# Sums of weight quarters: by VectorE subtractions before, by accumulating transfers from GpSimd after

## The chip, the cores and the metric

The kernel runs on one core of one Trainium2 chip. The metric is the device time of one execution, in microseconds (us). Before the change it is 1552.88 us, the median of 3 runs (1552.12 to 1553.69). The engines are TensorE (PE: matrix products; PEld is its weight load), VectorE (DVE), ScalarE (ACT), GpSimd (POOL) and SyncE (SP). Products are summed in PSUM; operands stand in SBUF. Transfers are carried out by 16 DMA engines and issued from the queue of an engine, in this kernel from SP and ACT.

## The reference

One layer of a decoder: a norm, two parallel token mixers fed by one input projection, an output projection, then a norm, a gated MLP with a causal convolution, and a last norm. There are 256 positions, D_MODEL is 2048 and D_FF is 5632, all in float32. The change lies in the last product, by w_down:

```python
h = rmsnorm(x, norm_ffn_w[l])
gate, up = jnp.split(jnp.einsum('bsd,df->bsf', h, w_up[l]), 2, axis=-1)
gate = causal_dwconv(gate, conv_ffn_w[l]) + conv_ffn_b[l]
x = x + jnp.einsum('bsf,fd->bsd', jax.nn.gelu(gate, approximate=False) * up, w_down[l])
return rmsnorm(x, norm_final_w)
```

## The kernel before

Float32 products are made of three products of parts: each operand is split into a high part (rounded to the type that TensorE takes) and a low part (what is left), and high times high, low times high and high times low are summed. A weight tile is [128, 2, 512], 256 rows of the weight by 512 columns, 512 KB. `srcs` is the list of all weight tiles in the order of their use. `load` issues the transfer of a tile on SP (line 157, four buffers `raw`). `begin` splits it: ScalarE casts it to the high part `whi` (line 209), then VectorE subtracts that from the tile, which gives `wlo` (line 217). `whi` and `wlo` have three buffers each, so a tile is split when TensorE has finished with the tile three places before. `weights` hands out the next tile and keeps two more split ahead (`AHEAD`).

The down projection is the last stage, from about 1311 us of the span. The activations are [256 positions, 5632], kept as 11 chunks of 512 features. It runs in two halves of 1024 output columns (`hf`), each with eight direct chunks and three chunks in `SEVEN`. A direct tile ("plain") is used for both position blocks: 12 matmuls. A chunk in `SEVEN` is a 2 by 2 by 2 block product made with seven products instead of eight: the weight block [512, 1024] of the chunk is loaded as two `quad` tiles of 1 MB (rows 0 to 255 and 256 to 511, line 167, buffers `x1` and `x2`), whose column halves are the quarters b11, b12, b21 and b22. The activations likewise have four blocks a11 to a22, and `half_sums` makes four sums of these, S1 to S4, and splits them.

The seven products come in the order of `PRODUCTS`: 11, 21, 22, T1, T3, T2, T4. The first three take a quarter as it is. For the others VectorE first replaces a quarter by a difference (line 204), in place: T1 in b11, T3 in b12, T2 in b22 and T4 in b21. The result is then split like any other tile. Each of the seven is used in 6 matmuls, and `stream` puts one plain tile behind each but the first. So a group is 11, 21, plain, 22, plain, T1, plain, T3, plain, T2, plain, T4, plain; there are three groups per half, six in all, with 4, 2 and 2 plain tiles ahead of the groups in the first half and 3, 1 and 1 in the second. Products 21, 22 and T4 are summed straight into the output's banks; 11, T1, T2 and T3 have banks of their own, which are combined once per half, after the last group (`u2`, `u3`, lines 1296 to 1304). A new group's quads are loaded when the buffers are free: the first when T1 and T3 of the group before are split, the second when T2 and T4 are.

The order of the instructions on each engine is set when the kernel is built, by a scheduler; each engine runs its list in order and waits on semaphores.

Of the kernel before, what the change touches and what calls it, by code (L numbers as in the profile page):

```python
# [12 lines left out]
ALU = mybir.AluOpType  # L13
# [22 lines left out]
def kernel(  # L36
# [20 lines left out]
    nc = tc.nc  # L57
# [11 lines left out]
    def nm(s):  # L69
        cnt[0] += 1  # L70
        return f"{s}_{cnt[0]}"

    def pg(shape=(P, 512)):
        return psg.tile(list(shape), F32, tag="g", name=nm("psg"))
# [70 lines left out]
    def weights(ahead=AHEAD):  # L145

        begin(taken[0] + ahead + 1)
        taken[0] += 1
        return made[taken[0] - 1]
# [11 lines left out]
    def quarter(half, chunk, what):  # L161

        if what == "11":
            for j in range(2):
                r = big.tile([P, 2, 1024], F32, tag=f"x{1 + j}", name=nm("quad"))
                rows = slice((2 * chunk + j) * 256, (2 * chunk + j + 1) * 256)
                last_load[0] = nc.sync.dma_start(r, w_down[0, rows, half * 1024 : (half + 1) * 1024]
                                                 .rearrange("(k p) f -> p k f", p=P)).ins
                for i in range(2):
                    quarters[j, i] = r[:, :, 512 * i : 512 * (i + 1)]  # L170
        b11, b12, b21, b22 = (quarters[j, i] for j in range(2) for i in range(2))
        sums = {"T1": (b11, b12, b11), "T3": (b12, b22, b12), "T2": (b22, b22, b11), "T4": (b21, b21, b22)}
        return sums[what] if what in sums else quarters[int(what[0]) - 1, int(what[1]) - 1]

    def load(n):
        while len(loads) < min(len(srcs), n):
            m = len(loads)
            for k in range(2) if m < HALVES else (slice(None),):
                load_part(m, k)
# [18 lines left out]
    def begin(n):  # L198
        while len(made) < min(len(srcs), n):
            load(len(made) + 1)  # L200
            raw = loads[len(made)]
            if isinstance(raw, tuple):
                raw, plus, minus = raw
                nc.vector.tensor_tensor(raw, plus, minus, op=ALU.subtract)
            shape = list(raw.shape)
            keep = kept.get(len(made))
            hi = wpool.tile(shape, F32R, tag="whi", name=nm("whi")) if keep is None else \
                mtile(keep, shape, F32R, nm("khi"))
            nc.scalar.copy(hi, raw)  # L209
            if shape[1] == 8:  # L210
                lo = None
                nc.vector.tensor_tensor(hi[:, :, 32:64], raw[:, :, 0:32], hi[:, :, 0:32].bitcast(F32),
                                        op=ALU.subtract)
            else:
                lo = wpool.tile(shape, F32R, tag="wlo", name=nm("wlo")) if keep is None else \
                    mtile(4 + keep, shape, F32R, nm("klo"))
                last_split[0] = nc.vector.tensor_tensor(lo, raw, hi.bitcast(F32), op=ALU.subtract).ins  # L217
                splits.append(last_split[0])
            made.append((hi, lo))
# [11 lines left out]
    def pm():  # L231
        return psm.tile([P, 2, 512], F32, tag="m", name=nm("psm"))
# [81 lines left out]
    def mtile(i, shape, dt, name):  # L314
        return big.tile(shape, dt, tag=f"m{i}", name=name)
# [207 lines left out]
    for g, w in enumerate(WINDOWS):  # L523
# [12 lines left out]
                            op=ALU.add)  # L536
# [29 lines left out]
    s1 = mp.tile([P, 2, NH], F32, name="s1")  # L566
# [3 lines left out]
    s2 = mp.tile([P, 2, NH], F32, name="s2")  # L570
# [602 lines left out]
    def half_sums(c):  # L1173

        h = whole[c]
        a11, a12, a21, a22 = (h[:, 2 * j : 2 * j + 2, t * P : (t + 1) * P] for t in range(2) for j in range(2))
        s = fp.tile([P, 4, S], F32, tag="y", name=nm("sums"))
        s1, s2, s3, s4 = (s[:, n].rearrange("p (k s) -> p k s", k=2) for n in range(4))
        nc.vector.tensor_tensor(s1, a21, a22, op=ALU.add)
        nc.vector.tensor_tensor(s2, s1, a11, op=ALU.subtract)  # L1180
        nc.vector.tensor_tensor(s3, a11, a21, op=ALU.subtract)
        nc.vector.tensor_tensor(s4, a12, s2, op=ALU.subtract)
        if c == SEVEN[1]:
            hi, lo = (lambda b: (b[:, 0], b[:, 1]))(big.tile([P, 2, 4, S], F32R, tag="x3", name="sx"))
        else:
            more = dict(tag="gs", bufs=2) if c == SEVEN[2] else {}
            hi, lo = (fp.tile([P, 4, S], F32R, name=f"s{n}{c}", **more) for n in ("hi", "lo"))
        nc.scalar.copy(hi, s)
        nc.vector.tensor_tensor(lo, s, hi.bitcast(F32), op=ALU.subtract)
        sums_of[c] = (hi, lo)  # L1190
# [53 lines left out]
    def products(ps, high, low, w, first, last, cs=slice(0, 512), shared=False):  # L1244
        for kk in range(2):
            for n, (part_, lhs) in enumerate(((w[0], high), (w[0], low), (w[1], high))):
                mm(ps[:, cs], lhs(kk), part_[:, kk, cs], start=(first and kk == 0 and n == 0),  # L1247
                   stop=(last and kk == 1 and n == 2), skip_group_check=shared)

    def direct(ps, kp, t, w, first, last, **more):  # L1250
        products(ps, lambda kk: lh(2 * kp + kk, t), lambda kk: ll(2 * kp + kk, t), w, first, last, **more)
# [4 lines left out]
    for hf in range(2):  # L1256
        if hf == 0:
            own = [pm() for c in range(2)]
            own = {(c, t): own[c][:, t] for c in range(2) for t in range(2)}
            other = [pg() for n in range(4)]  # L1260
        else:
            own = {(c, t): pg() for c in range(2) for t in range(2)}
            other = [p[:, t] for p in (pm(), pm()) for t in range(2)]
        bank_of = dict(zip(("11", "T1", "T2", "T3"), other))
        bank_of |= {"21": own[0, 0], "22": own[1, 0], "T4": own[0, 1]}
        began = set()
        for n, step in enumerate(steps[hf]):
            w = weights()
            if step[0] == "keep":
                wk.append(w)  # L1270
                continue
            if step[0] == "plain":
                kp, c = step[1], step[2] % 2
                more = any(x[0] == "plain" and x[2] % 2 == c for x in steps[hf][n + 1 :]) or hf == 1
                for t in range(2):
                    direct(own[c, t], kp, t, w, (c, t) not in began, not more, shared=hf == c == t == 1)
                    began.add((c, t))
                continue
            chunk, what = step[1:]
            if hf == 0 and what == "11" and chunk != SEVEN[-1]:  # L1280
                half_sums(SEVEN[SEVEN.index(chunk) + 1])
            which = OPERAND[what]
            if isinstance(which, tuple):
                high, low = (lambda kk, f=f, j=which[0], t=which[1], chunk=chunk: f(4 * chunk + 2 * j + kk, t)
                             for f in (lh, ll))
            else:
                high, low = (lambda kk, s=s, which=which: s[:, which, kk * P : (kk + 1) * P] for s in sums_of[chunk])
            ps = bank_of[what]
            alone = what in ("11", "T1", "T2", "T3")
            products(ps, high, low, w, alone and what not in began, alone and chunk == SEVEN[-1])  # L1290
            began.add(what)
            if chunk == SEVEN[-1] and what == PRODUCTS[-1]:
                c0, c1 = 2 * hf, 2 * hf + 1
                u = fp.tile([P, 2, 512], F32, tag="y", name=nm("u"))
                u2, u3 = u[:, 0], u[:, 1]
                nc.scalar.copy(u2, bank_of["11"])
                plus(0, c0, bank_of["11"])
                nc.vector.tensor_tensor(u2, u2, bank_of["T2"], op=ALU.add)
                nc.vector.tensor_tensor(u3, u2, bank_of["T3"], op=ALU.add)
                plus(1, c0, u3)  # L1300
                nc.vector.tensor_tensor(u2, u2, bank_of["T1"], op=ALU.add)
                plus(0, c1, u2)
                nc.vector.tensor_tensor(u3, u3, bank_of["T1"], op=ALU.add)
                plus(1, c1, u3)
        if hf == 0:
            for c in range(2):
                for t in range(2):
                    plus(t, c, own[c, t])
                    squared(t, c, c)
                    weighted(t, c)  # L1310
# [90 lines left out]
```

## Time and profile before

| What | Value |
|---|---|
| Median of 3 runs | 1552.88 us (1552.12 to 1553.69) |
| The profiled execution | 1552.15 us |
| Its span in the profile | 1550.4 us |
| Down projection's first matmul | at 1311.3 us of the span |
| VectorE's operations on line 204 | 24, each 1.22 us |
| Loads of quads | 12, 1 MB each |
| Issues from GpSimd's queue | none |

The profile is one execution. Its page has the busy time of each engine (a matmul counts from its start to a modelled end, so neighbours overlap), the span in 40 slices, the chain of work that ended last, the costliest groups of instructions and the transfers. Other views of the same trace are used too: the timeline (start and duration in us, engine, line, operation, output and inputs, and in brackets the idle time before it and what ended it), busy times in stretches of the span, a line's instructions with what its engine waited for (in total us, times), and the transfers by line with their size and the median time from issue to landing.

### The profile page before, as it was taken

The page shows a single profiled execution, that of the slowest core. Times are in us where ns is not written, and L with a number is a line of the kernel's source. Part 1 is how long each engine was busy: PE and PEld are TensorE (multiplying, and loading weights), DVE is VectorE, ACT ScalarE, POOL GpSimd, SP SyncE. Part 2 cuts the span into 40 slices and gives each one's busy share as a digit, 9 for nine tenths or more (in the row PEclk, how much of TensorE's full clock was granted, in tenths as well). Part 3 has the DMA queues.
Part 4 walks back from the last instruction along what each step waited for, and adds up shares of the span by engine and source line. Part 5 has one row for each costly group of instructions (what it writes and reads, how often), then busy time and mean ns, then how long its engine had stood idle before and what let it go on. Part 6 is the DMA issues. An engine that isn't in the chain of part 4 may idle for free.

```text
span 1550.4 us, 21200 instructions
## 1 busy us (share of the span) xinstructions
PE 1541.6 (99%) x7942; PEld 1294.1 (83%) x7942; DVE 1151.4 (74%) x1749; ACT 770.3 (50%) x987; POOL 39.3 (3%) x54
## 2 busy tenths in 40 slices
PE   9999999999999999999999999999999999999998
PEld 8888888788888888888888888888888888888886
DVE  6788858996689858886656667767666677877885
ACT  6445446454545446454554544444444444555552
POOL 1010001000100000000000000000000000000000
PEclk9999999999999999999999999999999999999999
DMA  8776757776576756675656666666666668557662
GB/s 274 214 219 206 204 152 223 215 209 183 170 237 202 208 164 202 217 206 175 215 181 185 187 186 188 189 190 189 184 195 186 187 189 271 176 190 231 201 209 93
DMA packets 165846, 306.34 MB, mean 198 GB/s; under 512 B 19138, under 2 KB 23010, under 8 KB 165614
## 3 DMA queue, kind: packets, MB, share of 16 engines
q1 hardware_dynamic: 162720, 299.95, 64.2%
q10 hardware_dynamic: 3022, 5.03, 1.0%
q8 instruction: 62, 1.02, 0.3%
q14 instruction: 42, 0.34, 0.1%
HBM read 299.66 MB, written 5.28 MB: 197 GB/s over the span
## 4 chain that ended last, share of the span: by engine, by line
PE 98%; issue 1%; DMA 1%; DVE 0%; ACT 0%; POOL 0%; POOLq 0%; ACTq 0%
PE psm L250 15%; PE psm L248 15%; PE psm L249 15%; PE psm L272 11%; PE psg L272 11%; PE psm L1247 7%; PE psg L1247 7%; PE psg L273 5%; PE psm L273 5%; PE psm L391 1%; PE psg L293 1%; PE psg L781 1%; PE psg L783 0%; DMA vrow<-ev 0%; PE psm L309 0%
## 5 line engine op out<-in xcount | busy, mean ns | idle before, releaser
L209 ACT CAST whi<-raw 128x1024 fp32r<-128x1024 f32 x500 | 526.0, 1052 | 612.9 <-PE psm L249 281.8
L217 DVE TENSOR_TENSOR wlo<-raw,whi 128x1024 fp32r<-128x1024 f32 x498 | 607.3, 1222 | 287.6 <-ACT whi L209 284.5
L250 PE MATMUL psm<-wlo,xhl 128*128 128x512 f32 x864 | 339.7, 393 | 0.6 <-DVE wlo L217 0.6
L248 PE MATMUL psm<-whi,xhl 128*128 128x512 f32 x864 | 338.6, 392 | 0.0
L249 PE MATMUL psm<-whi,xhl 128*128 128x512 f32 x864 | 337.9, 391 | 0.0
L272 PE MATMUL psm<-fhl,whi 128*128 128x512 f32 x704 | 246.1, 396 | 0.0
L272 PE MATMUL psg<-fhl,whi 128*128 128x512 f32 x704 | 238.2, 395 | 0.0
L273 PE MATMUL psm<-fhl,wlo 128*128 128x256 f32 x704 | 194.3, 279 | 0.0
L250 PEld LDWEIGHTS psm<-wlo,xhl 128*128 128x128 f32 x864 | 162.2, 188 | 35.1 <-DVE wlo L217 1.9
L249 PEld LDWEIGHTS psm<-whi,xhl 128*128 128x128 f32 x864 | 162.3, 188 | 33.4
L248 PEld LDWEIGHTS psm<-whi,xhl 128*128 128x128 f32 x864 | 162.3, 188 | 33.3 <-issue 0.2
L273 PE MATMUL psg<-fhl,wlo 128*128 128x256 f32 x704 | 178.9, 280 | 0.0
L272 PEld LDWEIGHTS psm<-fhl,whi 128*128 128x128 f32 x704 | 131.3, 188 | 30.4
L272 PEld LDWEIGHTS psg<-fhl,whi 128*128 128x128 f32 x704 | 129.2, 188 | 24.3
L273 PEld LDWEIGHTS psg<-fhl,wlo 128*128 128x128 f32 x704 | 132.5, 188 | 6.9
L273 PEld LDWEIGHTS psm<-fhl,wlo 128*128 128x128 f32 x704 | 132.6, 188 | 1.2
L209 ACT CAST whi<-quad 128x1024 fp32r<-128x1024 f32 x42 | 44.3, 1054 | 47.5 <-PE psm L1247 27.6
L217 DVE TENSOR_TENSOR wlo<-quad,whi 128x1024 fp32r<-128x1024 f32 x42 | 51.3, 1222 | 18.0 <-ACT whi L209 17.3
L1247 PE MATMUL psm<-whi,hhi 128*128 128x512 f32 (+1 forms) x150 | 58.0, 387 | 0.0
L1247 PE MATMUL psm<-whi,hlo 128*128 128x512 f32 (+1 forms) x150 | 58.0, 386 | 0.0
L1247 PE MATMUL psm<-wlo,hhi 128*128 128x512 f32 (+1 forms) x150 | 57.8, 386 | 0.0
L248 PE MATMUL psm<-whi,mhi 128*128 128x512 f32 x128 | 50.9, 397 | 0.0
(323 smaller groups left out, 1699.4 us busy)
## 6 DMA issues: line engine op xcount, KB each, us to landing
raw<-in_w_in_dram SPq DMA_DIRECT2D x224, 512.0 KB, 4.2
raw<-in_w_up_dram SPq DMA_DIRECT2D x176, 512.0 KB, 4.5
raw<-in_w_down_dram SPq DMA_DIRECT2D x64, 512.0 KB, 4.6
raw<-in_w_out_dram SPq DMA_DIRECT2D x32, 512.0 KB, 3.8
quad<-in_w_down_dram SPq DMA_DIRECT2D x12, 1024.0 KB, 6.2
mv<-vrow SPq DMA_DIRECT2D x12, 512.0 KB, 4.4
taps<-in_conv_qkv_w_dram SPq DMA_DIRECT2D x16, 256.0 KB, 6.5
raw<-in_pool_w_dram SPq DMA_DIRECT2D x8, 512.0 KB, 3.9
```

Source lines behind the costliest of these rows:

```text
L209: nc.scalar.copy(hi, raw)
L217: last_split[0] = nc.vector.tensor_tensor(lo, raw, hi.bitcast(F32), op=ALU.subtract).ins
L248: mm(ps[:, t, :], lh(k, t), hi[:, kk, :], start=(k == 0), stop=False)
L249: mm(ps[:, t, :], ll(k, t), hi[:, kk, :], start=False, stop=False)
L250: mm(ps[:, t, :], lh(k, t), lo[:, kk, :], start=False, stop=(k == nk - 1))
L272: mm(ps[f], hi[:, kk, fs], rhl(k), start=(k == 0), stop=False, skip_group_check=True)
L273: mm(ps[f][:, 1, :], lo[:, kk, fs], rhl(k)[:, 0, :], start=False, stop=(k == nk - 1), skip_group_check=True)
L293: nc.tensor.transpose(pt[:, ff, t * P : (t + 1) * P], src[:, t, f * P : (f + 1) * P], ident)
L391: mm(ps_k0[:, t, :], part(k, t), w[:, kk, :], start=(k == 0 and w is hi and part is xh), stop=(k == KD - 1 and w is lo))
L781: mm(pg0, kq[:, h, 0, 0:P], kq[:, h, :, :], start=True, stop=True)
L1247: mm(ps[:, cs], lhs(kk), part_[:, kk, cs], start=(first and kk == 0 and n == 0), stop=(last and kk == 1 and n == 2), skip_group_check=shared)
```

## The change

The four differences become sums, each added in place by a transfer from GpSimd's queue that accumulates onto its destination. The signs are moved to the sums of the activations (S1 and S4) and to the combination at the end of each half. The seven products, their order in `PRODUCTS`, the loads, the splits and the matmuls are as before. The third element of the tuples in `quarter` goes away, since the first quarter is now both operand and destination: T1 = b11 + b12 in b11, T3 = b12 + b22 in b12, T2 = b22 + T1 in b22, T4 = b21 + T2 in b21.

```diff
@@ in quarter
-        sums = {"T1": (b11, b12, b11), "T3": (b12, b22, b12), "T2": (b22, b22, b11), "T4": (b21, b21, b22)}
+        sums = {"T1": (b11, b12), "T3": (b12, b22), "T2": (b22, b11), "T4": (b21, b22)}
@@ in begin
             if isinstance(raw, tuple):
-                raw, plus, minus = raw
-                nc.vector.tensor_tensor(raw, plus, minus, op=ALU.subtract)
+                raw, other = raw
+                nc.gpsimd.dma_start(raw, other, accum_op=ALU.add)
@@ in half_sums
-        nc.vector.tensor_tensor(s1, a21, a22, op=ALU.add)
+        nc.vector.tensor_tensor(s1, a21, a22, op=ALU.subtract)
         nc.vector.tensor_tensor(s2, s1, a11, op=ALU.subtract)
         nc.vector.tensor_tensor(s3, a11, a21, op=ALU.subtract)
-        nc.vector.tensor_tensor(s4, a12, s2, op=ALU.subtract)
+        nc.vector.tensor_tensor(s4, a12, s2, op=ALU.add)
@@ at the end of each half
-                nc.vector.tensor_tensor(u2, u2, bank_of["T1"], op=ALU.add)
+                nc.vector.tensor_tensor(u2, bank_of["T1"], u2, op=ALU.subtract)
                 plus(0, c1, u2)
-                nc.vector.tensor_tensor(u3, u3, bank_of["T1"], op=ALU.add)
+                nc.vector.tensor_tensor(u3, bank_of["T1"], u3, op=ALU.subtract)
                 plus(1, c1, u3)
```

## The prediction

> **What bounds the kernel now.** I read the page first, for the engine that has no idle time.
>
> ```profile
> span 1550.4 us, 21200 instructions
> PE 1541.6 (99%) x7942; PEld 1294.1 (83%) x7942; DVE 1151.4 (74%) x1749; ACT 770.3 (50%) x987; POOL 39.3 (3%) x54
> PEclk9999999999999999999999999999999999999999
> PE 98%; issue 1%; DMA 1%; DVE 0%; ACT 0%; POOL 0%; POOLq 0%; ACTq 0%
> ```
>
> TensorE is busy 99% of the span at full granted clock and is 98% of the chain of waits. The change touches only the down projection, from about 1311 us on, so I asked for the busy times of that stage in stretches of 30 us, for the twelve plus twelve vector operations that the change takes away, and for what TensorE waits for on its line there.
>
> ```profile
> 1310.00:1340.00 30.00, 30.00 (x136) 24.76 (x135) 29.10 (x34) 17.86 (x20) 0.00 (x0) 1.00 0.52 175
> 1340.00:1370.00 30.00, 30.00 (x134) 24.86 (x133) 22.14 (x19) 15.84 (x15) 0.00 (x0) 1.00 0.64 214
> ...
> 1490.00:1520.00 30.00, 30.00 (x134) 24.86 (x133) 26.25 (x27) 16.64 (x17) 0.00 (x0) 1.00 0.52 172
> ```
>
> ```profile
> L204 DVE TENSOR_TENSOR quad<-quad x12: 1216/1224/1228, 1319.9 to 1498.6; 128x1024 f32<-128x1024 f32 x12
> L204 DVE TENSOR_TENSOR quad<-quad,quad x12: 1215/1218/1226, 1323.3 to 1497.3; 128x1024 f32<-128x1024 f32 x12
> ```
>
> ```profile
>   ACT whi L209: 0.4, 2
>   DVE wlo L217: 0.4, 2
> ```
>
> In the stretches the columns are TensorE, its weight loads, VectorE, ScalarE and GpSimd busy, then the clock, the DMA share and GB/s. TensorE is busy for all of each stretch, and in the whole stage it waits 0.8 us for split weights. So nothing that VectorE sheds is worth time here, and the stage has no reserve either: a microsecond that TensorE once waits is not won back, because it has no idle time to win it from.
>
> **What is removed.** 24 subtractions of 1.22 us are 29.3 us of VectorE. They lie beside TensorE work (the stretches above), so I count them at 0. Removing them could return at most the 0.8 us of waits.
>
> **What is added.** 24 transfers, four per group, issued by GpSimd, each adding one 512 KB quarter onto another. GpSimd's queue has nothing else in this stage (0.00 in the stretches), so nothing is held up behind them but the two tiny operations at the end. But the four form a chain: T1 adds b12 to b11, T3 then overwrites b12, T2 reads the new b11 and overwrites the b22 that T3 read, T4 reads the new b22. In the built kernel's instruction order every second, third and fourth transfer of a group waits for the one before to land, and the first for the VectorE half of quarter 11's split, since it overwrites that quarter. The question is how long one link L, from issue to the issue of the next, may be. The timeline of the second group gives it: VectorE's split of 11 and of 22, ScalarE's casts of T1, T3, T2 and T4, VectorE's split of T4, and TensorE's first matmuls on T4.
>
> ```profile
> 1349.15 1.23 DVE L217 TENSOR_TENSOR wlo<-quad,whi 128x1024 fp32r<-128x1024 f32 x1 [1.27 <-ACT whi L209]
> ...
> 1355.95 1.23 DVE L217 TENSOR_TENSOR wlo<-quad,whi 128x1024 fp32r<-128x1024 f32 x1
> ...
> 1372.27 1.22 DVE L217 TENSOR_TENSOR wlo<-quad,whi 128x1024 fp32r<-128x1024 f32 x1 [1.49 <-ACT whi L209]
> ```
>
> ```profile
> 1359.17 1.06 ACT L209 CAST whi<-quad 128x1024 fp32r<-128x1024 f32 x1 [1.89 <-PE psm L1247]
> ...
> 1363.02 1.05 ACT L209 CAST whi<-quad 128x1024 fp32r<-128x1024 f32 x1 [1.66 <-PE psm L1247]
> ...
> 1367.10 1.05 ACT L209 CAST whi<-quad 128x1024 fp32r<-128x1024 f32 x1 [1.21 <-PE psm L1247]
> ...
> 1371.18 1.05 ACT L209 CAST whi<-quad 128x1024 fp32r<-128x1024 f32 x1 [1.66 <-PE psm L1247]
> ```
>
> ```profile
> 1375.29 0.39 PE L1247 MATMUL psm<-whi,hhi 128*128 128x512 f32 x1
> 1375.52 0.39 PE L1247 MATMUL psm<-whi,hlo 128*128 128x512 f32 x1
> 1375.74 0.39 PE L1247 MATMUL psm<-wlo,hhi 128*128 128x512 f32 x1
> ```
>
> The split of 11 ends at 1349.15 + 1.23 = 1350.38. The casts of T1, T3, T2 and T4 start 8.8, 12.6, 16.7 and 20.8 us later, released by TensorE giving a buffer back. Each has a cushion before TensorE suffers: T4's low half must be done when its first low matmul starts at 1375.74, and it ends at 1372.27 + 1.22 = 1373.49, so the cast may come 2.25 us later. The chain is therefore free as long as L is at most 11.0 us for T1, 2L at most 14.9 for T3, 3L at most 19.0 for T2 and 4L at most 23.05 for T4. (The split of 22, done at 1357.18, is over before 2L for any L above 3.4 us.) T4 decides: the limit is L = 5.76 us, and beyond it TensorE stalls 4L − 23.05 per group, whether the wait shows at T2 or at T4. What is late next in a stall, on ScalarE behind the waiting cast, is the next plain tile, which TensorE needs only after the late one. The last group has the same measure, 1510.06 − 1489.26 = 20.8 us:
>
> ```profile
> 1488.03 1.23 DVE L217 TENSOR_TENSOR wlo<-quad,whi 128x1024 fp32r<-128x1024 f32 x1
> ```
>
> ```profile
> 1510.06 1.05 ACT L209 CAST whi<-quad 128x1024 fp32r<-128x1024 f32 x1 [1.62 <-PE psg L1247]
> ```
>
> So I take all six groups alike: the change costs 24L − 138 us for L above 5.76, and nothing below. SyncE's queue also hangs on the chain: the reload of the second pair of quarters waits for T4's split, and plain loads queue behind it. When T4 is late, TensorE is late too, so in the first three groups this is free; in the last three, with one plain tile between groups, it may add some tenths, which I leave out.
>
> **What is L?** No accumulating transfer and none issued by GpSimd stands in the trace, so I bound it by the nearest rows, transfers by size with their median time from issue to landing, and GpSimd's smallest operation in this stage.
>
> ```profile
> raw<-in_w_down_dram SPq DMA_DIRECT2D x64, 512.0 KB, 4.6
> raw<-in_w_out_dram SPq DMA_DIRECT2D x32, 512.0 KB, 3.8
> quad<-in_w_down_dram SPq DMA_DIRECT2D x12, 1024.0 KB, 6.2
> vrow<-ev SPq DMA_DIRECT2D x4, 512.0 KB, 4.4
> ```
>
> ```profile
> L1365 POOL TENSOR_TENSOR rsf<-rsf,epsx 128x1 f32<-128x1 f32 x2 | 1.1, 550 | 722.0 <-DVE rsf L1363 722.0
> ```
>
> Lower end: the addition comes free within a plain 512 KB copy, 3.8 us. Upper end: the destination is fetched, and only then written, in two passes of 4.4 us, 8.8 us, and more if it also shares the engines. Between them: an addition must fetch two operands of 512 KB, so it is nearest to the 1024 KB load of the same stage, 6.2 us. GpSimd makes its descriptors in software; I add 0.5 us for that, from its 0.55 us operation. I take L = 6.7 us, nearer to the 1024 KB row than to either end, because two operands must pass in any case while the wait between the passes is a guess.
>
> The sum: 24 × 6.7 − 138 = 22.8 us on the profiled execution's 1552.15 us (span 1550.4), 1575 us; the median of the runs, 1552.88, is 0.7 above that execution, which changes nothing at this size. The other edits are free: the signs in the four sums of activations and the operand order in the combination leave the same number of instructions of the same size.
>
> The Trainium skill has one more doubt about the length of a link: "SBUF — State Buffer", section "Who interferes with whom", says that GpSimd can be shut out of making descriptors while VectorE runs in a mode that takes both ports, and that an operation with two tensor inputs has no such mode. The VectorE rows of this stage are of that kind, so by this rule nothing is added; without the exemption a transfer could wait out one operation of 1.22 us, and the sum would be 24 × 7.9 − 138 = 52 us instead of 23.
>
> **Rivals.** First, *the transfers are hidden*: L stays under 5.76 us. For it: the shortest 512 KB landing is 3.8 us and a second 512 KB costs 6.2 − 4.6 = 1.6 us, together 5.4 us; source and destination both lie on the chip. Against it: GpSimd's own share, and that these transfers run beside the weight stream. The time is then 1552.9, not slower, with at most 0.8 us to gain. It decides as soon as L is under 5.8. The Trainium skill gives this case its figures: "DMA: Bandwidth & Descriptors", section "Anatomy of one DMA — SWDGE (gpsimd) path", fits 2.0 us plus bytes over 436 GB/s, and "Collectives: The Full Stack", section "The bandwidth ceiling: the fold count and why AG ≠ RS ≠ AR", says that a reducing transfer costs twice the reads and no time for the addition; an estimate from both is 2.0 + 2 × 1.2 = 4.4 us, hidden. No row here shows such a transfer.
>
> Second, *the links are long*, 7.5 to 10 us: either the two passes of 8.8 us, or the engines fill up. The DMA share of the stretches is 0.52 to 0.64 in the rows shown; four links of twice 1.6 us of all engines per 30 us add 0.43, which is about 1, so the weight stream and the links would stretch each other. At L = 8.8 the cost is 73 us: 1626. Against it: plain transfers beside the same stream keep 4.6 us.
>
> Third, *faster*: VectorE is full in the first stretch (29.10 of 30), and freeing it could end the 0.8 us of waits. Even all of it gives 1552.1, so a gain of 0.2% would need something the profile does not show.
>
> **How the numbers follow.** Links of 5.9 to 7.5 us, the forecast: 0.40, own range 1556 to 1595. Hidden: 0.28. Long: 0.28, of which about 0.12 lies above L = 9.0 (1630). Faster by over 0.2%: 0.04. 0.2%, 3.1 us, is about what a measurement of this kernel can tell from no change, so L must pass 5.9 to count as slower: 0.40 + 0.28 = 0.68; same 0.28; faster 0.04. The range reaches from the hidden case, 1551, to L = 9.0, 1630.
>
> **What would show it.** If the steps are right, TensorE shows waits for the high halves of T2 and T4 in each of the six groups, ScalarE's casts of quarters name a DMA as releaser, GpSimd's issues within a group are about 6.7 us apart, and stretches before 1311 us are unchanged. If the issues are less than 5.7 us apart and TensorE still has 30.00 of 30, the hidden case holds; if also T1's cast is late, or casts of plain tiles wait for loads, links are past 11 us or the stream is starved. VectorE must lose about 29 us without TensorE gaining any. The forecast fails if L is on the other side of 5.8, or if TensorE stalls by another amount than four times L less 23 per group.

## The result, and the profile after

The changed kernel takes 1607.34 us (median of 4 runs, 1606.52 to 1608.03) beside 1553.24 us for the kernel before in runs on the same chip: a ratio of 1.0349, 95% interval 1.0331 to 1.0367, or 54 us more. The forecast was 1575: the side is right, the loss is more than twice the 22 us forecast. The first rows are from the page: span, busy times, granted clock in 40 slices, the queue of GpSimd's transfers (packets, MB, share), the chain that ended last by engine, and the rows of ScalarE's casts of quarters and of GpSimd's issues.

```profile
span 1606.0 us, 21235 instructions
PE 1560.3 (97%) x7942; PEld 1300.3 (81%) x7942; DVE 1123.0 (70%) x1725; ACT 768.0 (48%) x987; POOL 73.7 (5%) x78
PEclk9999999999999999999999999999999999999899
q0 software_dynamic: 6528, 12.58, 4.5%
PE 85%; DMA 9%; issue 3%; DVE 1%; ACT 1%; POOLq 0%; POOL 0%; ACTq 0%; DVEq 0%; SPq 0%
L209 ACT CAST whi<-quad 128x1024 fp32r<-128x1024 f32 x42 | 44.1, 1050 | 115.7 <-DMA quad<-quad 84.5
L204 POOL DMA_DIRECT2D quad<-quad x24 | 28.7, 1195 | 712.2 <-DMA raw<-in_w_down_dram 498.2
quad<-quad POOLq DMA_DIRECT2D x24, 512.0 KB, 6.6
```

VectorE shed 28.4 us (1151.4 to 1123.0) and the span grew by 55.6. The chain, 98% TensorE before, is 9% transfers now. ScalarE waits 84.5 us for the accumulating transfers before it can cast a sum. The median from issue to landing is 6.6 us, which is almost the 6.7 of the forecast; so the median is not what went wrong.

In the view of waits from 1345 to 1562 us, TensorE (columns: us in total, times, longest) stands still for ScalarE's casts, in the two kinds of output banks, and hardly for VectorE:

```profile
PE psm L1247 <- ACT whi L209: 19.4, 5, 6.5
PE psg L1247 <- ACT whi L209: 14.0, 5, 7.6
PE psm L1247 <- DVE wlo L217: 0.5, 1, 0.5
```

The first group shows where. From four timelines: VectorE's split of quarter 11 (1.22 us from 1319.29, the start of the chain), GpSimd's four issues T1, T3, T2 and T4, two of SyncE's issues, and ScalarE's casts of the four sums.

```profile
1319.29 1.22 DVE L217 TENSOR_TENSOR wlo<-quad,whi 128x1024 fp32r<-128x1024 f32 x1
```

```profile
1320.83 1.37 POOL L204 DMA_DIRECT2D quad<-quad  x1 [498.16 <-DMA raw<-in_w_down_dram]
1326.34 1.21 POOL L204 DMA_DIRECT2D quad<-quad  x1 [4.14 <-DMA quad<-quad]
1334.29 1.18 POOL L204 DMA_DIRECT2D quad<-quad  x1 [6.74 <-DMA quad<-quad]
1339.70 1.19 POOL L204 DMA_DIRECT2D quad<-quad  x1 [4.23 <-DMA quad<-quad]
```

```profile
1339.56 0.37 SPq L167 DMA_DIRECT2D quad<-in_w_down_dram  x1
1340.02 3.33 SPq L157 DMA_DIRECT2D raw<-in_w_down_dram  x2
```

```profile
1328.96 1.06 ACT L209 CAST whi<-quad 128x1024 fp32r<-128x1024 f32 x1 [0.35 <-PE psm L1247]
...
1333.85 1.05 ACT L209 CAST whi<-quad 128x1024 fp32r<-128x1024 f32 x1 [2.88 <-DMA quad<-quad]
...
1339.51 1.05 ACT L209 CAST whi<-quad 128x1024 fp32r<-128x1024 f32 x1 [3.65 <-DMA quad<-quad]
...
1350.59 1.04 ACT L209 CAST whi<-quad 128x1024 fp32r<-128x1024 f32 x1 [9.09 <-DMA quad<-quad]
```

The four links take 5.5, 8.0, 5.4 and 10.9 us. The last is the long one, and SyncE's rows say what is beside it: 0.14 us before GpSimd issues T4's transfer, SyncE issues the 1 MB reload of the first pair of quarters, and two plain loads behind it (at 1340.02 and 1342.98). Both the reload and T4's transfer wait for the same event, T2's landing. T4's cast comes 1350.59 − 1320.51 = 30.08 us after 11's split; the limit of the prediction was 23.05. TensorE's timeline at that place:

```profile
1345.20 0.39 PE L1247 MATMUL psm<-wlo,hhi 128*128 128x512 f32 x1
1351.69 0.80 PE L1247 MATMUL psm<-whi,hhi 128*128 128x512 f32 x1 [6.10 <-ACT whi L209]
1352.28 0.63 PE L1247 MATMUL psm<-whi,hlo 128*128 128x512 f32 x1
```

It stands for 6.1 us, close to 30.08 − 23.05 = 7.0. The matmul behind the wait takes 0.80 us instead of 0.39, and the next 0.63: in a view of stretches the granted clock is 0.77 from 1345 to 1360 (columns: TensorE, weight loads, VectorE, ScalarE, GpSimd busy, clock, DMA share, GB/s), and 1.00 again in the next.

```profile
1345.00:1360.00 15.00, 8.86 (x31) 6.45 (x30) 5.83 (x5) 5.04 (x5) 0.00 (x0) 0.77 0.77 225
1360.00:1385.00 25.00, 25.00 (x112) 20.54 (x110) 12.20 (x11) 10.43 (x10) 4.72 (x4) 1.00 0.82 208
```

The same picture stands in the first five groups, with waits of 6.1, 6.5, 6.1, 7.6 and 5.8 us at T4. The last group has no reload behind it, and its T4 link alone is short, 5.2 us; its longest wait is 1.28 us, at T2.

### The profile page after: what moved, and what is told of

It is laid out like the page before. It is cut to its first block, busy times and chain, and to the rows that moved or that the text cites. A ratio compares the mean times of both kernels' runs of the same rounds, so it can differ in the third digit from the quotient of the medians.

```text
span 1606.0 us, 21235 instructions
## 1 busy us (share of the span) xinstructions
PE 1560.3 (97%) x7942; PEld 1300.3 (81%) x7942; DVE 1123.0 (70%) x1725; ACT 768.0 (48%) x987; POOL 73.7 (5%) x78
## 4 chain that ended last, share of the span: by engine, by line
PE 85%; DMA 9%; issue 3%; DVE 1%; ACT 1%; POOLq 0%; POOL 0%; ACTq 0%; DVEq 0%; SPq 0%
PE psm L250 14%; PE psm L248 14%; PE psm L249 14%; PE psm L272 10%; PE psg L272 10%; DMA quad<-quad 8%; PE psm L273 5%; PE psg L273 5%; PE psg L1247 3%; PE psm L1247 3%; PE psm L391 1%; PE psg L293 1%; DMA quad<-in_w_down_dram 1%; PE psg L781 1%; DVE wlo L217 1%
## 5 line engine op out<-in xcount | busy, mean ns | idle before, releaser
L250 PEld LDWEIGHTS psm<-wlo,xhl 128*128 128x128 f32 x864 | 162.3, 188 | 35.7 <-DVE wlo L217 2.6
L272 PEld LDWEIGHTS psm<-fhl,whi 128*128 128x128 f32 x704 | 131.3, 188 | 30.3
L272 PEld LDWEIGHTS psg<-fhl,whi 128*128 128x128 f32 x704 | 129.3, 188 | 24.2
L209 ACT CAST whi<-quad 128x1024 fp32r<-128x1024 f32 x42 | 44.1, 1050 | 115.7 <-DMA quad<-quad 84.5
L1247 PE MATMUL psg<-whi,hhi 128*128 128x512 f32 (+1 forms) x130 | 53.3, 410 | 14.5 <-ACT whi L209 14.5
L204 POOL DMA_DIRECT2D quad<-quad x24 | 28.7, 1195 | 712.2 <-DMA raw<-in_w_down_dram 498.2
```

The lines of the kernel that those rows point to most:

```text
L204: nc.gpsimd.dma_start(raw, other, accum_op=ALU.add)
L250: mm(ps[:, t, :], lh(k, t), lo[:, kk, :], start=False, stop=(k == nk - 1))
L272: mm(ps[f], hi[:, kk, fs], rhl(k), start=(k == 0), stop=False, skip_group_check=True)
```

## Experiments

Each kernel is a small edit of the changed one, or two edits combined. None beats the kernel before; the first two equal it. Ratios are against the kernel before on the same chip, with 95% intervals. The theory that grew out of the trace: the loss is the chain of four transfers ending too late, and T4's link is the long one because the reload goes ahead of it.

### All four sums back on VectorE

```diff
-                nc.gpsimd.dma_start(raw, other, accum_op=ALU.add)
+                nc.vector.tensor_tensor(raw, raw, other, op=ALU.add)
```

> All 24 additions go back to VectorE, in the new form with plain additions. Contended-chain theory (the loss is the lateness of the four linked transfers beyond 23.05 us per group, and T4's link is long because the reload of the first quad, released at the same instant, runs ahead of it) and long-link theory (accumulating transfers take 7 us or more whatever runs beside them) both expect 1553 us, within 2 us. If the new signs or the moved order of instructions cost anything, part of the 54 us stays.

Measured: 1553.31 us, ratio 1.0000 (0.9991 to 1.0009), as expected. The form with plain additions, the moved signs and the other order of instructions cost nothing. The whole loss is in how the sums are made.

### Only T4's sum by a transfer

```diff
+                nc.vector.tensor_tensor(raw, raw, other, op=ALU.add) if srcs[len(made)][2] != "T4" else
                 nc.gpsimd.dma_start(raw, other, accum_op=ALU.add)
```

> T1, T3 and T2 by VectorE, T4 alone by a transfer, which can start some 10 us earlier than its cast needs it. Both theories of lateness: hidden even at 11 us, 1553 to 1555 us. If a transfer costs time as such, by slowing TensorE or the weight stream, a quarter of the loss stays: 1566 us.

Measured: 1552.80 us, ratio 1.0002 (0.9991 to 1.0012). One accumulating transfer per group, 6.3 us from issue to landing in the median, costs nothing at all when its operands are ready early. A transfer is no loss; a chain of them can be.

### The reload after T4's landing

```diff
+                if j == 0 and last_sum[0] is not None:
+                    tc.add_manual_dep(last_load[0], last_sum[0].name, AFTER, reason="after_t4")
...
-                nc.gpsimd.dma_start(raw, other, accum_op=ALU.add)
+                last_sum[0] = nc.gpsimd.dma_start(raw, other, accum_op=ALU.add).ins
```

> All transfers stay; only the reload of the first quad waits until T4's transfer has landed. Contended-chain theory: T4's link falls from about 11 us to about 5.5 us, the chain to 5.4 + 7.9 + 5.4 + 5.5 = 24.2 us, 1.2 us over the limit per group, no long stall and no half clock: 1560 us (1555 to 1570). Long-link theory: the chain keeps its length of about 29 us, and the later reload can only add: 1607 us or more.

Measured: 1587.43 us, ratio 1.0214 (1.0197 to 1.0232). T4's link fell as expected; in the first group its cast comes 24.2 us after 11's split. But the time missed 1560, as the reloads are late in their turn. In the second half there is one plain tile between groups, and ScalarE's timeline shows first the cast of the fourth group's T4, then the casts of the next 11 and 21 waiting for the reloads:

```profile
1471.06 1.05 ACT L209 CAST whi<-quad 128x1024 fp32r<-128x1024 f32 x1 [3.34 <-DMA quad<-quad]
...
1476.82 1.05 ACT L209 CAST whi<-quad 128x1024 fp32r<-128x1024 f32 x1 [2.82 <-DMA quad<-in_w_down_dram]
1482.65 1.04 ACT L209 CAST whi<-quad 128x1024 fp32r<-128x1024 f32 x1 [4.78 <-DMA quad<-in_w_down_dram]
```

So the reload has a place where it must not come (ahead of T4's transfer) and a time by which it must.

### The reload issued right behind T4's transfer

The same idea without the wait: GpSimd issues the first pair's reload, behind T4's transfer in its own queue. (Line numbers behind the edit are one higher.)

```diff
+                own = j == 0 and last_sum[0] is not None
-                last_load[0] = nc.sync.dma_start(r, ...).ins
+                last_load[0] = (nc.gpsimd if own else nc.sync).dma_start(r, ...).ins
+                if own:
+                    tc.add_manual_dep(last_load[0], last_sum[0].name, BEHIND, reason="behind_t4")
```

> The reload of the first pair of quarters is issued by GpSimd right behind T4's transfer, not by SyncE 0.1 us ahead of it; all else as in the changed kernel. Theory (what is issued first goes first): T4's link falls from 11 to 5.5-7.5 us, its cast comes 24 to 26 us after 11's split, TensorE waits 1 to 3 us per group and keeps its clock mostly, 1562 to 1580. Rival (a 1 MB load in flight beside it slows the transfer whatever the order): the link stays at 9 us or more and the time at 1595 to 1607.

Measured: 1581.10 us, ratio 1.0175 (1.0160 to 1.0191), 1.1 us above the 1562 to 1580 expected. GpSimd's timeline and ScalarE's cast of T4:

```profile
1332.20 1.17 POOL L205 DMA_DIRECT2D quad<-quad  x1 [6.11 <-DMA quad<-quad]
1338.56 1.21 POOL L205 DMA_DIRECT2D quad<-quad  x1 [5.18 <-DMA quad<-quad]
1339.29 1.22 POOL L166 DMA_DIRECT2D quad<-in_w_down_dram  x1
```

```profile
1344.28 1.04 ACT L210 CAST whi<-quad 128x1024 fp32r<-128x1024 f32 x1 [3.92 <-PE psm L1248]
```

The reload is still issued beside T4's transfer, 0.7 us behind it instead of 0.14 ahead. T4's cast follows its issue by 5.7 us, not 10.9, and is released by TensorE giving a buffer back, so the transfer had landed by then. Bytes, number of transfers and VectorE's work are the same. That is 26 of the 54 us, and it decides against the rival: a reload in flight hardly slows T4's transfer; one issued ahead of it does. The edit also moves the reload into GpSimd's queue, so by the times alone order and queue are not told apart. The view of the DMA queues (packets, MB, share of the 16 engines) shows what happens. In the changed kernel, from 1340.70 to 1344.70, only q1, the queue of SyncE's loads, moves data, 1.01 MB, which is the size of the reload; T4's packets, on GpSimd's queue q0, come from 1344.70 to 1349.90:

```profile
q1 hardware_dynamic: 268, 1.01, 85.9%
...
q0 software_dynamic: 267, 0.52, 54.1%
q1 hardware_dynamic: 441, 0.88, 50.7%
```

What the same load would do if SyncE issued it right behind T4's transfer, no run shows. With the reload behind on GpSimd's queue, T4's packets move soon after their issue and nearly alone, from 1339.60 to 1343.50:

```profile
q0 software_dynamic: 252, 0.51, 89.3%
q1 hardware_dynamic: 2, 0.00, 0.0%
```

### T4's sum on VectorE, twice

First with T4's sum simply given to VectorE, then with that sum queued behind the last split ahead of it (the edit puts the three transfers behind a split in the same way):

```diff
+                with tc.issue_after(last_split[0]):
+                    nc.vector.tensor_tensor(raw, raw, other, op=ALU.add) if srcs[len(made)][2] == "T4" else
-                nc.gpsimd.dma_start(raw, other, accum_op=ALU.add)
+                    nc.gpsimd.dma_start(raw, other, accum_op=ALU.add)
```

> T1, T3 and T2 by transfers, T4 by VectorE. Contended-chain theory: the chain up to T2 is 5.4 + 7.9 + 5.4 = 18.7 us against a limit of 19.0, so 1553 to 1557 us. Long-link theory with equal links of 7.4 us: 22.2 us, 3.2 us over in each of six groups, 19 us and more: 1572 us or above.

> As with T4's sum on VectorE before, but queued on VectorE behind the last split ahead of it, so that it cannot stand there waiting for T2's transfer in front of other splits. Theory (the loss comes from T4's late link; the earlier attempt failed by VectorE's order alone): T2 lands 17 to 20 us after 11's split, the sum takes 1.2 us, T4's cast is within its limit of 23.05, time 1553 to 1560. Rival (three transfers per group in this stage cost by themselves, through the DMA engines): it stays near the 1600 of the earlier attempt, at least 1580.

Measured: 1600.42 us, ratio 1.0305 (1.0289 to 1.0320), more than 40 us above the 1553 to 1557 expected; and 1570.96 us, ratio 1.0112 (1.0095 to 1.0128). VectorE's timeline of the first shows why it failed:

```profile
1328.99 1.22 DVE L217 TENSOR_TENSOR wlo<-raw,whi 128x1024 fp32r<-128x1024 f32 x1
1337.15 1.23 DVE L204 TENSOR_TENSOR quad<-quad 128x1024 f32<-128x1024 f32 x1 [6.94 <-DMA quad<-quad]
1338.29 1.22 DVE L217 TENSOR_TENSOR wlo<-quad,whi 128x1024 fp32r<-128x1024 f32 x1
1339.43 1.22 DVE L217 TENSOR_TENSOR wlo<-raw,whi 128x1024 fp32r<-128x1024 f32 x1
```

The scheduler put T4's sum ahead of T3's split. VectorE stands there 6.94 us for T2's transfer, with splits behind it whose high halves are ready, and TensorE's waits name VectorE instead of ScalarE:

```profile
PE psm L1247 <- DVE wlo L217: 28.3, 5, 8.0
```

Queued in turn, that row shrinks to 0.5 us in one wait, and 29 us come back. It still missed the 1553 to 1560 expected: three links alone end 19.5 us after 11's split, past T2's own limit of 19.0, and the sum then waits for two splits ahead of it, so T4's cast comes at 24.0 to 25.0 in the first four groups and 28.5 in the last two.

### Three links in the chain instead of four

T2 is summed in T1's place, so it waits for T1's split and not for T3's transfer.

```diff
-        sums = {..., "T2": (b22, b11), "T4": (b21, b22)}
+        sums = {..., "T2": (b11, b22), "T4": (b21, b11)}
```

> T2 is summed in the place of T1 (11's quarter plus 22's) and T4 reads it from there, so T2 waits for T1's split but no longer for T3's transfer; T1, T2, T4 are the chain, T3 stands beside it, and both reloads now come only after T4. Theory (number of links and what is issued between them): T2 issued about 11 us after 11's split, T4 about 17, landing at 22 to 23.5, T4's wait 0 to 1 us; the first pair's reload is then as late as in the run with the reload after T4, but about 2 us earlier than there, so 1556 to 1575. Rival (the last transfer is slow wherever it stands): T4's link keeps about 11 us and the time stays at 1595 or more.

Measured: 1572.63 us, ratio 1.0126 (1.0111 to 1.0141), within what the theory had. In the first group T4's cast comes 5.1 us after its issue (1338.30 to 1343.37), with no reload ahead; the later reloads cost in the last groups, where T4's cast is 26.6 and 29.6 us behind 11's split.

### Plain copies

```diff
-                nc.gpsimd.dma_start(raw, other, accum_op=ALU.add)
+                nc.gpsimd.dma_start(raw, other)
```

> The 24 transfers from GpSimd stay in place but copy instead of adding (the four sums of each group are left out: T1 to T4 then hold the copied quarter). Theory that an addition fetches two operands and so doubles the data time of a link: a link that runs alone falls from 5.4 us to about 4.2 us, the chain by about 5 us to 25 us, 2 us over the limit per group: about 1565 to 1575 us. Theory that the addition itself is free and a link is issue, start and waiting behind loads: links and time as in the changed kernel, 1607 us.

Measured: 1563.35 us, ratio 1.0069 (1.0042 to 1.0096), just under the 1565 to 1575 of the first theory and far from the 1607 of the second. The kernel leaves out the sums, so only its time is of use. GpSimd's timeline:

```profile
1319.86 0.91 POOL L204 DMA_DIRECT2D quad<-quad  x1 [498.14 <-DMA raw<-in_w_down_dram]
1323.66 0.73 POOL L204 DMA_DIRECT2D quad<-quad  x1 [2.90 <-DMA quad<-quad]
1327.56 0.72 POOL L204 DMA_DIRECT2D quad<-quad  x1 [3.16 <-DMA quad<-quad]
1334.45 0.72 POOL L204 DMA_DIRECT2D quad<-quad  x1 [6.17 <-DMA quad<-quad]
```

A copy's first link is 3.80 us where an addition's is 5.51 (1320.83 to 1326.34): adding costs 1.7 us in this link, of which 0.46 is GpSimd's longer issue (1.37 for 0.91). At 3.8 us for every link the chain would be far under its limit; but T2's takes 6.9 us, and T4's cast comes 7.6 us after its issue (1342.01); here too SyncE issues the reload 0.14 us ahead of T4's transfer (1334.31).

### Half transfers, alone and with the reload behind

```diff
-                nc.gpsimd.dma_start(raw, other, accum_op=ALU.add)
+                [nc.gpsimd.dma_start(raw[:, k], other[:, k], accum_op=ALU.add) for k in range(2)]
```

The second kernel has this and the edit of the reload behind T4's transfer.

> Each addition is issued as two transfers of half the quarter, so that the first half of a link can start when the first half of the one before it has landed. Theory (the chain is latency, four links one after the other): half links of 3 to 4 us, T4 lands within 20 us of 11's split, and its issue is no longer behind the reload; 1553 to 1560. Rival (the DMA engines or GpSimd are the limit: twice as many issues of 0.7 to 1.2 us and the same bytes): links as long as before, 1595 to 1615.

> Both edits together: half transfers, and the first pair's reload issued by GpSimd behind T4's second half. Theory (T4's cast past its limit of 23.05 us after 11's split, summed over the groups, is the loss): without the reload in front, T4's second half lands 5 us after its issue, so its cast comes 22 to 24 us after 11's split, 0 to 1 us over the limit per group; with some microseconds for the later reload 1556 to 1572. Rival (cost per issue or per byte of 48 transfers): 1580 or more, as with half transfers alone.

Measured: 1586.82 us, ratio 1.0207 (1.0190 to 1.0225), between the 1553 to 1560 of the theory and the 1595 to 1615 of the rival; and together with the reload issued by GpSimd 1568.38 us, ratio 1.0102 (1.0085 to 1.0118), within 1556 to 1572. Halves shorten the first links, but T4's second half is issued when T2's second half has landed, the moment at which SyncE issues the reload. In the first group SyncE's reload is at 1338.19 and that half at 1338.33, and its cast follows only at 1346.80, 8.5 us for 256 KB. With the reload behind, the same half takes 1341.19 − 1337.14 = 4.1 us.

### Three transfers of four

T1's sum on VectorE, the other three by transfers, the reload behind T4's (that edit is left out below).

```diff
+                last_sum[0] = (nc.vector.tensor_tensor(raw, raw, other, op=ALU.add) if srcs[len(made)][2] == "T1" else
+                               nc.gpsimd.dma_start(raw, other, accum_op=ALU.add)).ins
```

> T1's sum on VectorE right behind 11's split, the other three by transfers, the first pair's reload by GpSimd behind T4's. Theory (a chain of four does not fit into 23.05 us, one of three does): 1.2 us for T1's sum, then links of about 7, 6 and 5.5 us, so T4's cast lies 20 to 22 us after 11's split, within its limit; the last two groups may lose 1 to 3 us each to the reload as before: 1553 to 1564. Rival (any chain of transfers beside the weight stream costs in proportion to its links): three quarters of the 28 us that four links with this reload cost, 1574.

Measured: 1558.38 us, ratio 1.0035 (1.0023 to 1.0047). Within the 1553 to 1564 expected, and far from the rival's 1574: three transfers per group, 18 in all, 6.4 us each in the median, cost 5.5 us. TensorE's waits in the stage:

```profile
PE psg L1249 <- DVE wlo L219: 1.6, 4, 0.5
PE psg L1249 <- ACT whi L211: 1.6, 3, 1.2
```

### The wait filled

24 matmuls by a tile of zeros ahead of T4's, in the first five groups, keep TensorE at work while T4's transfer is under way (`zero` is that tile, `tail` the high half of the tile before).

```diff
...
+            if what == "T4" and (hf, chunk) != (1, SEVEN[-1]):
+                for n2 in range(FILL):
+                    mm(ps, zero, tail[:, 0, :], start=False, stop=False, skip_group_check=True)
```

> 24 extra matmuls by a tile of zeros stand ahead of T4's products in the first five groups, 5.4 us of work each at full clock, which adds zero to the bank and fits into the waits of 6.0 to 7.8 us there. Theory with a clock term (TensorE comes back from a wait of over 3 us at half clock, about 15 us of the 54): the waits stay as long, but no half clock follows, so the time falls to about 1593 us although 120 matmuls (27 us) are added. Theory without it (the waits alone make the loss): 1607 us as in the changed kernel, or more.

Measured: 1607.65 us, ratio 1.0354 (1.0337 to 1.0370): no gain. TensorE's timeline in the third group, where the clock stayed at 1.00:

```profile
1426.12 5.60 PE L1297 MATMUL psm<-whi,zero 128*128 128x512 f32 x24
1431.90 0.50 PE L1247 MATMUL psm<-whi,hhi 128*128 128x512 f32 x1 [0.18 <-ACT whi L209]
...
1433.16 0.50 PE L1247 MATMUL psm<-wlo,hhi 128*128 128x512 f32 x1 [0.53 <-DVE wlo L217]
...
1439.94 0.50 PE L1247 MATMUL psm<-wlo,hhi 128*128 128x512 f32 x1 [1.57 <-DVE wlo L217]
```

The matmuls behind T4's cast run at full speed and then wait for VectorE, whose splits are as late as the cast was. In the waits from 1345 to 1562 us these are 5.4 us, where the changed kernel has 0.5: there the slow matmuls seem to cover them.

```profile
PE psm L1247 <- DVE wlo L217: 3.7, 5, 1.6
PE psg L1247 <- DVE wlo L217: 1.7, 3, 0.6
```

In the first two groups the clock fell all the same, 5 us later, behind the filling, although the longest wait there is 1.0 us. So the half clock is no term that could be taken off the loss by itself; what it costs beside those waits stays open.

## Why the prediction was right or wrong

**No reserve in the stage, VectorE's 29 us worth nothing: right.** VectorE lost 28.4 us and TensorE gained none. All sums on VectorE, or one of four by a transfer, both give the time of before.

**The limit of 23.05 us for T4's cast after 11's split: right in the first four groups.** Across the runs, casts within it go with no loss and later ones with more. The table takes the distance from the end of VectorE's split of 11 to ScalarE's cast of T4 in each group from the two timelines, sums what lies above 23.05, and sets beside it the span above the 1550.4 us of before.

| Kernel | T4's cast after 11's split, six groups, us | Sum above 23.05 | Span above before |
|---|---|---|---|
| T4 alone by a transfer | 20.2, 20.8, 20.8, 20.4, 21.1, 20.2 | 0 | -0.5 |
| all sums on VectorE | 20.7, 20.8, 20.8, 20.4, 21.7, 20.3 | 0 | 1.6 |
| three transfers of four | 21.4, 20.8, 20.8, 23.4, 25.7, 23.8 | 3.7 | 7.5 |
| plain copies | 22.5, 26.3, 23.2, 24.1, 25.2, 21.9 | 6.7 | 10.2 |
| halves, reload behind | 22.3, 25.6, 23.2, 24.1, 28.2, 27.5 | 13.4 | 15.8 |
| three links | 23.5, 25.2, 25.2, 23.1, 26.6, 29.6 | 14.9 | 24.1 |
| T4 on VectorE, in turn | 24.2, 24.1, 25.0, 24.0, 28.5, 28.4 | 15.9 | 18.3 |
| reload behind T4 | 25.2, 26.9, 27.2, 26.3, 27.7, 27.3 | 22.3 | 26.7 |
| reload after T4's landing | 24.2, 26.0, 26.0, 24.7, 29.5, 30.4 | 22.5 | 35.7 |
| halves | 26.9, 26.6, 27.1, 27.3, 29.7, 28.1 | 27.4 | 38.1 |
| T4 on VectorE, first | 27.7, 30.9, 29.6, 25.8, 32.2, 29.2 | 37.1 | 50.9 |
| the wait filled | 30.3, 31.0, 29.6, 30.9, 34.6, 27.2 | 45.3 | 54.1 |
| the changed kernel | 30.1, 30.5, 30.3, 31.8, 33.6, 28.4 | 46.3 | 55.6 |

The order of the losses follows the sum but for one pair, and in the changed kernel the sum is 83% of the loss. The limit was read from the second group and taken for all six. In the changed kernel's first four, TensorE's long wait is 0.9 to 1.1 us less than what lies above it; in the last two it is 5.8 and 1.3 us where 10.6 and 5.3 lie above it, so there 11's split is no longer a good start to measure from, and the 83% is in part luck.

**One length L = 6.7 us for all four links: this step failed.** It is the step "I take L = 6.7 us", sized from the 1024 KB load, and with it "24 × 6.7 − 138 = 22.8". A link with no load issued just ahead of it takes 5.4 to 5.5 us in the first group, under the limit of 5.76, so four of these would have stayed hidden; the median is 6.6. But a chain pays the sum, and in the first group the sum has two long members: T4's, 10.9 us (5.2 in the last group, where no reload follows), and T3's, 8.0. The six chains add up to 184.6 us, a mean of 7.7 per link, and 24 × 7.7 − 138 gives 47 instead of 23: this term was too small by a microsecond, which is 24 of the 32 us that the forecast fell short. The cause of T4's share is shown: the reload's packets go first, and with the reload behind, its 10.9 become 5.7 and 26 us return. That T3's comes from plain loads in flight beside it (their median to landing rose from 4.6 to 5.8 us) was not tried by itself. The queues fit it: T1's packets move from 1322.5 to 1326.3 us with nothing else moving, while between 1328.5 and 1334.2 T3's share the engines with 0.69 MB of loads, one of them issued 0.6 us ahead of T3's transfer (1325.75).

**SyncE's queue: the wrong pair.** The prediction followed the reload of the second pair, which waits for T4's split, and left it out. The reload that costs is the first pair's. Before, no sum was a transfer, so none could be issued beside it; now T2's landing releases it and T4's transfer at once. Nor were the last groups worse by "some tenths": the first three exceed the limit by 7.0 to 7.4 us, the fourth and fifth by 8.7 and 10.6, the last by 5.3.

**What a stall costs: not in the sum.** The prediction let a stall cost its own length. TensorE's waits in the stage add up to 36.5 us (0.8 before), and its busy time for the same 7942 matmuls grew by 18.7 us (1541.6 to 1560.3); together that is 54.4 of the 55.6 us. Behind each long wait the clock falls to half, and splits queued behind the late cast are late too. The filled wait, which won nothing, suggests that the two cover each other; their shares are open.

**The rivals.** Hidden transfers: its link length was real, 5.5 us for the first link, but only with no load just ahead. The Trainium skill's figures behind it, "DMA: Bandwidth & Descriptors", section "Anatomy of one DMA — SWDGE (gpsimd) path", with the doubled reads and the free addition of "Collectives: The Full Stack", section "The bandwidth ceiling: the fold count and why AG ≠ RS ≠ AR", came to an estimate of 4.4 us. The first link here took 5.51, 1.7 more than a plain copy, 0.46 of it GpSimd's longer issue; whether the rest is the second read, no run separates. Long links: the measured time lies in its range and above the forecast's own 1556 to 1595, and the mean link of 7.7 us in its 7.5 to 10. Of its two mechanisms the passes of 8.8 us do not fit, since a link can take 5.4; loads and links stretching each other fits better, though for T4 it is one load ahead and not engines that are full on average. The doubt about VectorE shutting GpSimd out, which came to 52 us, has the size of the loss and not its cause: the reload's order alone returns half with VectorE's work unchanged.

**What would show it.** Casts released by a transfer, VectorE's loss and the unchanged start of the stage (1312.1 us, before 1311.3) came as said. Issues 6.7 us apart did not: 5.5, 8.0 and 5.4. Nor did waits at both T2 and T4: T2's cast in the first group stood at 1339.51, 19.0 us after 11's split, exactly its limit; in the next three it comes at 18.8 to 19.3 and in the last two at 22.9 and 23.0, and still all long waits are at T4.

## What to carry to other kernels

A chain of transfers pays the sum of its links, so a median says little; take each link, and ask of each what the landing before it also releases. A bulk load that becomes free at the moment when an urgent transfer does is better issued behind it: here, moving it from 0.14 us ahead to 0.7 us behind, in the transfer's own queue, was worth 26 us. An operation that waits on a transfer belongs late in an in-order queue, or it makes everything behind it wait too.

## What the runs showed of the hardware

TensorE's granted clock fell to half behind each of the five long waits of the changed kernel, and the matmuls behind them took 0.63 us instead of 0.39 for some microseconds. It also fell behind five waits with half transfers, where the longest is 3.5 us, and behind none with three of four, where the longest is 1.2. The Trainium skill, "TensorE: Matmul & The Clock Gate", section "What's actually happening", has half rate after an idle window of about 3.4 us that runs freely; the traces agree for the long waits. But the clock also fell behind a wait of 1.9 us with the reload behind T4 and behind waits of 1.0 us in the filled kernel, and not behind one of 2.4 us with plain copies, so here the measured clock does not follow that window alone. A transfer that GpSimd issues occupies it 1.19 us when it adds 512 KB, 0.72 when it copies them, 0.85 when it adds 256 KB.
